# A feed-forward layer as five blocks of seven products, with the plain unit inside the first

## The chip, the cores and the metric
The kernel runs on one core of a Trainium2 chip. The metric is the device time of one execution in microseconds: the median of three runs before is 913.37 us (912.84 to 914.23). Time is also read from one execution recorded by the hardware profiler.

## What is computed
Two layers over 256 tokens of width 1024. Each layer has a SwiGLU feed-forward network (FFN), a mixer (an mLSTM in layer 0, windowed attention in layer 1) and a second FFN, each followed by a layer norm over the scaled residual. Everything is fp32. The part that matters here is the FFN, above all the last of the four:

```
def swiglu(x, w_in, w_out):          # x 256 x 1024, w_in 1024 x 5632, w_out 2816 x 1024
    gu = x @ w_in
    g, u = gu[..., :D_FF], gu[..., D_FF:]
    return (jax.nn.silu(g) * u) @ w_out
...
x = layer_norm(ALPHA * x + 0.5 * swiglu(x, ffn_w_in[l, 1], ffn_w_out[l, 1]), ln_g[l, 2], ln_b[l, 2])
```

## The kernel before
**Precision.** Every matmul operand is split into a high and a low part. ScalarE rounds a weight piece (128 x 1024 numbers) to the high part (`w_hi`), VectorE subtracts to get the low part (`w_lo`); both come from the raw piece in `w_raw` or `s_raw`. A product is then three matmuls: high by high, high by low, low by high (`mm3`, line 617). The tokens' side (x transposed, `xT_hi` and `xT_lo`) stands in the array, the weights stream through with 512 columns. The weights can be split at most `RING` = 10 pieces ahead.

**An FFN in 11 units.** The 2816 hidden columns are 11 units of 256. Before, each FFN does the first two units plainly (512 columns of g and 512 of u: 96 matmuls, eight pieces, each used for both token halves), then one unit plainly (`beside`: 256 columns of g next to 256 of u in one piece: 48 matmuls, four pieces), then four blocks of two units each by a scheme of seven products (Strassen's). `down` multiplies a finished 128-row chunk of the hidden layer by one piece of `w_out`: 12 matmuls per chunk, into four PSUM banks `py` that stay open to the end; six chunks are left for the `tail`, in which the layer norm starts as the halves finish.

**A block of seven products.** The weight block is cut in halves by rows of x (0 to 511, 512 to 1023) and by g and u columns: b11 and b21 for g, b12 and b22 for u, each as two pieces. x is cut by tokens and by columns; four sums of x (S1 to S4, `x_sum`, line 845) are made once per FFN. A block needs, in the order in which TensorE uses them: b11 (with x itself), b21 (with x), t1 (b11 after one sum, with S1), t2 (after a second sum, with S2), b12 after a sum (with S3), b22 (with S4), b11 after a third sum (with x). That is 14 split pieces and 84 matmuls. The sums of weights are made partly by VectorE (`sum`, line 348, which adds one raw piece to another) and partly by DMA (`add`, line 121: POOL issues a transfer from DRAM that is added to the piece in place). The raw pieces of b11, b12, b22 lie in rooms `s_raw0` to `s_raw3`, two pieces per room, with b11 in `s_raw0` and `s_raw3` by turns. PSUM bank qa collects the products with x (tokens half 0), S2, S3 and at last x (half 1); it is copied or read between them.

**What sets the order.** The code that plans the pieces (line 492 and after) writes down the order in which pieces are split and the due times. When the kernel is built, a planner (`Paced`, `Weights.fill`, lines 65 and 376) follows the engines with its own estimates of time and puts each split, sum and late eviction at a place between the other instructions. On the chip the engines' queues are then fixed: every engine takes its instructions in the order in which they were built and waits by semaphores. SP issues the loads of weights in order; POOL issues the DMA additions in order, between its small arithmetic.

**At the border to the last FFN.** During the attention (`attn`, line 1335) the rooms `s_raw1` and `s_raw2` hold the attention's probabilities and `s_raw3` its keys. The second token half of x is normalised late; `pending()` transposes it into xT once it is ready, so the FFN begins with token half 0 and calls `pending()` after 42 of its matmuls. S1 to S4 need both halves.

Of the kernel before, what the change touches and what calls it, by code (L numbers as in the profile page):

```python
# [21 lines left out]
F = 2816  # L22
UNITS = F // 256
SEVENS = 4
RAW_BUFS = 4
S_RAW = 2
# [162 lines left out]
class Weights:  # L189
# [5 lines left out]
    def __init__(self, nc, pool, rooms, words, plan, after):  # L195
        self.nc, self.pool, self.rooms, self.words, self.plan, self.after = nc, pool, rooms, words, plan, after
        self.raw, self.parts, self.half, self.sums = {}, {}, [], []
        self.made, self.used, self.gone, self.left = set(), 0, 0, 0
        self.todo = {tag: [i for i, w in enumerate(words) if w["tag"] == tag] for tag in TAGS}
        self.free = {"v_raw": 0, **{tag: S_RAW for tag in TAGS}, "w_raw": RAW_BUFS}  # L200
        self.spool, self.send, self.span = None, 0, FIRST
        self.later, self.fresh, self.owed, self.landed = [], None, 0, False
        self.uses = [0] * len(words)
# [19 lines left out]
    def load(self, most=None):  # L223
# [4 lines left out]
        while most is None or n < most:  # L228
            next_ = []
            for tag, todo in self.todo.items():  # L230
                if not todo:
                    continue
                first = self.first[todo[0]]
                if tag != "w_raw":
                    if self.free[tag] and not once and first < self.used + self.span:
# [209 lines left out]
def trunk_kernel(ctx: ExitStack, tc: tile.TileContext, x, ffn_w_in, ffn_w_out, ln_g, ln_b, ml_w_in, ml_gate_b,  # L445
# [45 lines left out]

    def seven(w, c0, c1, n, down):

# [5 lines left out]
        b21 = at(512, c0)  # L499
        full = n < SEVENS - 1  # L500
# [24 lines left out]

    ends = {}
    for j, (kind, l, i, _) in enumerate(stages):
        if kind == "ffn":
# [6 lines left out]

            for c0 in (0, F):
                for a in range(4):
                    wide(wi, a * 256, c0)
            for a in range(4):
                beside(wi, a * 256, 512, F + 512)  # L540
            down(2)
            for g in range(SEVENS):
                c0 = 768 + 512 * g
                seven(wi, c0, F + c0, g, down)
            down(6)
# [224 lines left out]
    def ffn(l, i, n, pending, last):  # L770
        with ExitStack() as ph:
# [96 lines left out]

            hB = h_room(4)
            chunks(hB, 4)  # L870
            hB0 = hB
            if start:
                sg = {}
# [71 lines left out]

            def seven(full, before):

# [36 lines left out]
                product(qa, of(0, 0), True, end1)  # L984
                before()
                if not full:
                    gb.extend(load_ln(lambda name: W.room(name, TAGS[1]), l, n))
# [5 lines left out]
                down(1)  # L993
                product(qa, sum_("S3"), False, end7)
                product(qb, sum_("S4"), False, end3)
                if full:
                    down(1)
                product(qa, of(4, 1), False, end4)
                if full:
                    down(1)  # L1000
# [6 lines left out]

            ps = [wbank(), wbank()]
            pieces = []
            for a in range(4):  # L1010
                pieces.extend(W.take(1))
                for t in range(2):
                    for k in (2 * a, 2 * a + 1):
                        mm3(ps[t], pair(xT, A, k, tok(t)), pair(pieces[a], A, k % 2), k == 0, k == 7)
                W.done()
                if not start:
                    for n_, f_ in zip(XP[1:], (x_three, x_two, x_four)):
                        if a == n_:
                            f_()
                if a == 1:  # L1020
                    for t in range(0 if start else 1, 2):
                        tr(hB0, t, hs[t])
            hh = []
            for t in range(2):
                sg = temp("sg")[:, 0:256]
                nc.scalar.activation(sg, ps[t][:, 0:256], AF.Silu)
                hh.append(temp("hh")[:, 0:256])
                nc.vector.tensor_mul(hh[t], sg, ps[t][:, 256:512])
            hp = h_room(2)
            chunks(hp, 2)  # L1030
            down(1)

            def turn():
                p = wbank((128, 2, S))
                for t in range(2):
                    for k in range(2):
                        nc.tensor.transpose(p[:, k, tok(t)], hh[t][:, k * 128:(k + 1) * 128], ident)
                split_evac(hp, p, wait=True)

            down(1)  # L1040
            for g in range(SEVENS):
                turn = seven(g < SEVENS - 1, turn)
            if start:
# [7 lines left out]
            return tail(y, lambda c, t: pair(hT[c], A, tok(t)), (todo, todo), False, norm,  # L1051
                        last, 4, turn, TAGS[1])

# [281 lines left out]
    def attn(l, n, pending, last):  # L1335
        with ExitStack() as ph:
# [215 lines left out]
            for st in range(11):  # L1552
# [83 lines left out]
```

## Time and profile before

| what | value |
|---|---|
| median of three runs | 913.37 us |
| the profiled execution's own time | 913.42 us |
| its span, first to last instruction | 911.7 us |
| TensorE busy, share of the span | 902.5 us, 99% |
| VectorE busy | 804.4 us, 88% |
| ScalarE busy | 573.1 us, 63% |
| POOL busy | 152.5 us, 17% |
| granted TensorE clock, mean | 0.999 |

In the rows, PE is TensorE's matmuls, PEld its weight loads, DVE is VectorE, ACT ScalarE, SP the engine that issues loads. A row of the timeline gives the start and the length in us, then engine, line, operation, output and inputs, shape, and how many instructions of that kind follow each other; in brackets the idle time before it and what ended it. A row of stretches gives, for a stretch of time, the busy time and the count of PE, PEld, DVE, ACT and POOL, then the granted clock, the DMA engines' busy share and the GB/s moved. Nearly all instructions are recorded in one helper (`call`, line 179), so they stand under L180 and are told apart by the names of their tiles. Busy times of pipelined instructions overlap a little; the spacing of starts is what one more of them costs.

### The profile page before, as it was taken

The page shows a single profiled execution, that of the slowest core. Times are in us where ns is not written, and L with a number is a line of the kernel's source. Part 1 is how long each engine was busy: PE and PEld are TensorE (multiplying, and loading weights), DVE is VectorE, ACT ScalarE, POOL GpSimd, SP SyncE. Part 2 cuts the span into 40 slices and gives each one's busy share as a digit, 9 for nine tenths or more (in the row PEclk, how much of TensorE's full clock was granted, in tenths as well). Part 3 has the DMA queues.
Part 4 walks back from the last instruction along what each step waited for, and adds up shares of the span by engine and source line. Part 5 has one row for each costly group of instructions (what it writes and reads, how often), then busy time and mean ns, then how long its engine had stood idle before and what let it go on. Part 6 is the DMA issues. An engine that isn't in the chain of part 4 may idle for free.

```text
span 911.7 us, 12563 instructions
## 1 busy us (share of the span) xinstructions
PE 902.5 (99%) x4459; PEld 757.4 (83%) x4459; DVE 804.4 (88%) x971; ACT 573.1 (63%) x793; POOL 152.5 (17%) x192
## 2 busy tenths in 40 slices
PE   9999999999999999999999999999999999999996
PEld 7888888889988888888888888888898888888885
DVE  5999999886799898999888899998869889899886
ACT  5776777356664656776646676764569566676660
POOL 0111123113211011212011111110425301111110
PEclk9999999999999999999999999999999999999999
DMA  8999998546637898997868989986534587899851
GB/s 281 367 328 259 288 274 215 162 137 186 208 111 246 296 234 244 290 285 234 241 193 269 259 257 283 272 223 197 159 119 140 163 293 221 204 298 278 252 138 47
DMA packets 100703, 208.53 MB, mean 229 GB/s; under 512 B 6904, under 2 KB 21264, under 8 KB 100640
## 3 DMA queue, kind: packets, MB, share of 16 engines
q1 hardware_dynamic: 82368, 173.04, 54.2%
q0 software_dynamic: 17696, 33.65, 22.3%
q10 hardware_dynamic: 576, 1.05, 0.3%
q8 instruction: 35, 0.57, 0.3%
q14 instruction: 28, 0.23, 0.1%
HBM read 206.65 MB, written 1.05 MB: 228 GB/s over the span
## 4 chain that ended last, share of the span: by engine, by line
PE 98%; DVE 1%; DMA 0%; issue 0%; DVEq 0%
PE pw L180 64%; PE py L180 35%; DMA x<-in_x_dram 0%; DVE x L180 0%; DVE stats L180 0%; DVEq L1632 0%; DVE mv L180 0%; DVE rs L180 0%
## 5 line engine op out<-in xcount | busy, mean ns | idle before, releaser
L180 DVE TENSOR_TENSOR w_lo<-w_raw,w_hi 128x1024 fp32r<-128x1024 f32 (+1 forms) x213 | 255.2, 1219 | 26.6 <-ACT w_hi L180 24.8
L180 ACT CAST w_hi<-w_raw 128x1024 fp32r<-128x1024 f32 (+1 forms) x213 | 218.9, 1049 | 80.3 <-PE py L180 21.7
L180 DVE TENSOR_TENSOR w_lo<-s_raw,w_hi 128x1024 fp32r<-128x1024 f32 x192 | 228.6, 1219 | 18.3 <-ACT w_hi L180 18.2
L180 ACT CAST w_hi<-s_raw 128x1024 fp32r<-128x1024 f32 x192 | 196.6, 1054 | 58.4 <-PE py L180 23.3
L180 PE MATMUL pw<-w_hi,xT_hi 128*128 128x512 f32 x480 | 189.5, 396 | 0.0
L180 PE MATMUL pw<-w_hi,xT_lo 128*128 128x512 f32 x480 | 187.0, 391 | 0.0
L180 PE MATMUL pw<-w_lo,xT_hi 128*128 128x512 f32 x480 | 186.7, 390 | 0.0
L122 POOL DMA_DIRECT2D s_raw<-in_ffn_w_in_dram x64 | 77.4, 1211 | 484.1 <-DVE s_raw L180 226.3
L180 PE MATMUL py<-w_hi,h_hi 128*128 128x512 f32 x349 | 138.2, 396 | 0.0
L180 PE MATMUL py<-w_hi,h_lo 128*128 128x512 f32 x349 | 136.2, 390 | 0.0
L180 PE MATMUL py<-w_lo,h_hi 128*128 128x512 f32 x349 | 136.0, 390 | 0.0
L180 PEld LDWEIGHTS pw<-w_hi,xT_lo 128*128 128x128 f32 x480 | 90.0, 188 | 19.1
L180 PEld LDWEIGHTS pw<-w_lo,xT_hi 128*128 128x128 f32 x480 | 90.3, 188 | 18.6 <-DVE w_lo L180 1.2
L180 PEld LDWEIGHTS pw<-w_hi,xT_hi 128*128 128x128 f32 x480 | 90.1, 188 | 17.4 <-ACT w_hi L180 0.2
L180 PE MATMUL pw<-w_hi,S_hi 128*128 128x512 f32 x256 | 99.7, 390 | 0.0
L180 PE MATMUL pw<-w_lo,S_hi 128*128 128x512 f32 x256 | 99.7, 389 | 0.0
L180 PE MATMUL pw<-w_hi,S_lo 128*128 128x512 f32 x256 | 99.7, 389 | 0.0
L180 PEld LDWEIGHTS py<-w_hi,h_lo 128*128 128x128 f32 x349 | 65.5, 188 | 14.1
L180 DVE TENSOR_TENSOR s_raw<-s_raw,s_raw 128x1024 f32<-128x1024 f32 x64 | 76.8, 1219 | 0.3
L180 PEld LDWEIGHTS py<-w_lo,h_hi 128*128 128x128 f32 x349 | 65.7, 188 | 13.0
L180 PEld LDWEIGHTS py<-w_hi,h_hi 128*128 128x128 f32 x349 | 65.6, 188 | 12.7
L180 PEld LDWEIGHTS pw<-w_hi,S_lo 128*128 128x128 f32 x256 | 48.1, 188 | 10.0
(205 smaller groups left out, 1122.7 us busy)
## 6 DMA issues: line engine op xcount, KB each, us to landing
s_raw<-in_ffn_w_in_dram SPq DMA_DIRECT2D x96, 512.0 KB, 8.0
w_raw<-in_ffn_w_out_dram SPq DMA_DIRECT2D x88, 512.0 KB, 6.1
w_raw<-in_ffn_w_in_dram SPq DMA_DIRECT2D x64, 512.0 KB, 5.7
s_raw<-in_ffn_w_in_dram POOLq DMA_DIRECT2D x64, 512.0 KB, 8.3
w_raw<-in_ml_w_in_dram SPq DMA_DIRECT2D x24, 512.0 KB, 4.6
w_raw<-in_ffn_w_in_dram SPq DMA_DIRECT2D x32, 256.0 KB, 6.0
w_raw<-in_at_w_in_dram SPq DMA_DIRECT2D x12, 512.0 KB, 4.8
w_raw<-in_ml_w_out_dram SPq DMA_DIRECT2D x8, 512.0 KB, 4.1
```

Of the source, the lines that this page charges most:

```text
L122: self.nc.gpsimd.dma_start(ap, source, accum_op=OP.add)
L180: r = f(out, *args, **kw)
```

## The change
Only the last FFN changes (stage 5, `FIVE`). Its hidden columns are taken as one plain 256-column unit and five blocks of seven products; the plain 512-column unit is gone. The plain unit no longer stands ahead of the blocks: it is `inner`, called within the first block between its second product (b21) and its third (S1), first for token half 0, with `pending()` in it, then for token half 1. The four sums of x are made in `inner` too, one after each quarter of token half 1 (`XF`). The transposes of the plain unit's result (`before()`), which in other blocks follow the first product, stand in this block after the product with S3, and right behind them the first `down`; the second follows the product with S4.

In the first block of the last FFN (`MOVED1`) the first sum of b11 is no longer made by VectorE from the b12 piece but by a DMA addition of the same columns from DRAM; b12's own addition then comes after t1's sum. The first block's b11 is loaded, split and added to during the attention. `W.lent` holds back loads into `s_raw1` and `s_raw2` while the attention uses these rooms. The result of the plain unit for both token halves lies in one 512-column temporary instead of two, and the last normalisation's g and b are loaded into the rooms `s_raw3` instead of `s_raw0`.

```diff
+FIVE = (5,)
+MOVED1 = ((5, 0),)
+XF = [0, 1, 2, 3]
...
         for j in range(2):
-            after[s1[j]] = [(b11[j], b12[j]), (b12[j], at(512, c1)[j])]
+            after[s1[j]] = [(b11[j], at(0, c1)[j] if (count, n) in MOVED1 else b12[j])]
+            if (count, n) not in MOVED1:
+                after[s1[j]].append((b12[j], at(512, c1)[j]))
...
-        down(1)
+        (inner or (lambda: down(1)))()
         t1 = [split_of(w_, None, p, half, BY_SUM) for w_, p in zip(b11, s1)]
         for j in range(2):
             after[t1[j]] = [(b11[j], b22[j])]
+            if (count, n) in MOVED1:
+                after[t1[j]].append((b12[j], at(512, c1)[j]))
...
+                for g in range(5):
+                    c0 = 256 + 512 * g
+                    seven(wi, c0, F + c0, g, down, 5, inner if g == 0 else None)
...
                 product(qa, of(0, 0), True, end1)
-                before()
+                if inner is None:
+                    before()
...
                 product(qc, of(4, 0), True, end2)
-                down(1)
+                if inner is None:
+                    down(1)
+                else:
+                    inner()
                 qb = wbank()
                 product(qb, sum_("S1"), True, end5)
                 product(qa, sum_("S2"), False, end6)
-                down(1)
+                if inner is None:
+                    down(1)
                 product(qa, sum_("S3"), False, end7)
+                if inner is not None:
+                    before()
+                    down(1)
                 product(qb, sum_("S4"), False, end3)
                 if full:
                     down(1)
                 product(qa, of(4, 1), False, end4)
-                if full:
+                if full and inner is None:
                     down(1)
...
+            def inner():
+                pieces = []
+                for t in range(2):
+                    ps = wbank()
+                    for a in range(4):
+                        if t == 0 and 2 * a == PEND[bound[0] - 1]:
+                            pending()
+                        if t == 0:
+                            pieces.extend(W.take(1))
+                        for k in (2 * a, 2 * a + 1):
+                            mm3(ps, pair(xT, A, k, tok(t)), pair(pieces[a], A, k % 2), k == 0, k == 7)
+                        if t == 1:
+                            W.done(W.used - 4 + a + 1)
+                            for n_, f_ in zip(XF, (x_one, x_three, x_two, x_four)):
+                                if a == n_:
+                                    f_()
+                    gated(t, ps)
...
+            W.lent = TAGS[2:4]
...
+            W.lent = ()
+            W.load()
```

More of the change, by code (lines that the diff above doesn't have):

```diff
@@ L234, in load @@
                 if tag != "w_raw":
-                    if self.free[tag] and not once and first < self.used + self.span:
+                    if self.free[tag] and tag not in self.lent and not once and first < self.used + self.span:
                         next_.append((first, tag, tag))
@@ L490, in rows, with seven @@
         piece(w[c * 128:(c + 1) * 128, :].rearrange("(k p) f -> p k f", p=128), 1, scale)
-    def seven(w, c0, c1, n, down):
+    def seven(w, c0, c1, n, down, count, inner=None):
         def at(r0, c):
@@ L499, in seven @@
         b21 = at(512, c0)
-        full = n < SEVENS - 1
+        full = n < count - 1
         half = 1360.0
@@ L944, in ffn, with seven @@
             gb = []
-            def seven(full, before):
+            def seven(full, before, inner=None):
                 of = lambda k0, t: (lambda k: pair(xT, A, k0 + k, tok(t)))
@@ L998, in seven @@
                 product(qa, of(4, 1), False, end4)
-                if full:
+                if full and inner is None:
                     down(1)
@@ L1006, in seven, with gated @@
                 return second
[L1008 to L1022, printed above, removed]
             hh = []
-            for t in range(2):
+            def gated(t, ps):
+                if t == 0:
+                    hh.append(temp("hh"))
                 sg = temp("sg")[:, 0:256]
[L1026 to L1031, printed above, removed]
+                nc.scalar.activation(sg, ps[:, 0:256], AF.Silu)
+                s_ = slice(256 * t, 256 * t + 256)
+                nc.vector.tensor_mul(hh[0][:, s_], sg, ps[:, 256:512])
             def turn():
@@ new lines, in ffn @@
+            if five:
+                hp = h_room(2)
+                chunks(hp, 2)
+            else:
+                ps = [wbank(), wbank()]
+                pieces = []
+                for a in range(4):
+                    pieces.extend(W.take(1))
+                    for t in range(2):
+                        for k in (2 * a, 2 * a + 1):
+                            mm3(ps[t], pair(xT, A, k, tok(t)), pair(pieces[a], A, k % 2), k == 0, k == 7)
+                    W.done()
+                    if not start:
+                        for n_, f_ in zip(XP[1:], (x_three, x_two, x_four)):
+                            if a == n_:
+                                f_()
+                    if a == 1:
+                        for t in range(0 if start else 1, 2):
+                            tr(hB0, t, hs[t])
+                for t in range(2):
+                    gated(t, ps[t])
+                hp = h_room(2)
+                chunks(hp, 2)
+                down(1)
+                down(1)
@@ L1043, in ffn @@
+            count = 5 if five else SEVENS
+            for g in range(count):
+                turn = seven(g < count - 1, turn, inner if five and g == 0 else None)
             if start:
```

49 lines of the change are left out of this document (30 added, 19 removed).

## The prediction
> **What bounds the kernel now.** I read the first part of the page (busy shares), then the chain of work that ended last, then the chain in order of time for the pace of one matmul, then the table of stretches and TensorE's waits over the last FFN, since only that FFN changes.
>
> ```profile
> span 911.7 us, 12563 instructions
> PE 902.5 (99%) x4459; PEld 757.4 (83%) x4459; DVE 804.4 (88%) x971; ACT 573.1 (63%) x793; POOL 152.5 (17%) x192
> PE 98%; DVE 1%; DMA 0%; issue 0%; DVEq 0%
> 56.70 5.44 PE pw L180 x24
> 729.50:887.00 157.50, 157.50 (x717) 130.46 (x717) 145.84 (x151) 103.97 (x124) 20.85 (x17) 1.00 0.85 244
> PEld pw L180 <- issue: 0.3, 2, 0.2
> ```
>
> TensorE is the chain: 98% of it, and from 729.5 to 887 us (the last FFN up to its tail) it is busy throughout; the only wait that TensorE's weight loads show from 700 us on is 0.3 us of issue. So a matmul taken away is a gain in full and a stall is a loss in full. One 512-column matmul costs 5.44 / 24 = 0.2267 us. The same row of the last FFN shows what is close behind: VectorE is busy 145.84 of 157.50 us, only 11.7 us idle. ScalarE (103.97) has room.
>
> **What goes: 12 matmuls.** A plain unit is 2 token halves x 2 column blocks x 8 rows of x x 3 = 96 matmuls, a block of seven products 7 x 4 x 3 = 84. Transposes are as many as before, and the built order of TensorE is 12 instructions shorter. Gain: 12 x 0.2267 = 2.72 us.
>
> **What comes on VectorE.** From the end of the attention's normalisation (the second `x<-x,rs,ln_b`) to the last `w_lo`, I count VectorE's built order by kind: 82 splits (`w_lo`) and 16 sums of 1024 columns before, 88 and 18 after (a block has 14 pieces where the unit had 8; of its four sums of weights two, those with b12, become DMA additions), and three 512-column steps more (five evictions for the two of the unit).
>
> ```profile
> 736.43 1.28 DVE L180 SCALAR_TENSOR_TENSOR x<-x,rs,ln_b 128x1024 f32<-128x1024 f32 x1
> 737.63 2.35 DVE L180 TENSOR_TENSOR w_lo<-w_raw,w_hi 128x1024 fp32r<-128x1024 f32 x2
> 808.31 4.62 DVE L180 TENSOR_TENSOR w_lo<-s_raw,w_hi 128x1024 fp32r<-128x1024 f32 x4
> 812.85 2.35 DVE L180 TENSOR_TENSOR w_lo<-w_raw,w_hi 128x1024 fp32r<-128x1024 f32 x2
> 762.07 0.69 DVE L180 TENSOR_TENSOR S_lo<-S,S_hi 128x512 fp32r<-128x512 f32 x1
> 762.67 0.68 DVE L180 TENSOR_TENSOR h_lo<-pw,h_hi 128x512 fp32r<-128x512 f32 x1
> 765.87 0.75 DVE L180 TENSOR_TENSOR hh<-sg,pw 128x256 f32<-128x256 f32 x2 [0.18 <-ACT sg L180]
> ```
>
> Back to back, one step of 1024 columns takes (812.85 - 808.31) / 4 = 1.135 us, one of 512 takes 0.60 (762.07 to 762.67), one of 256 about 0.35. Added: 8 x 1.135 + 3 x 0.60 = 10.9 us, against 11.7 us idle before. In total it fits, barely; so the question is where in time it falls. [...]
>
> **Where it falls: the first block.** Before, the plain 512-column unit gave VectorE and ScalarE 96 matmuls in which few pieces were due. Now the first block's sums, the four sums of x (S1 to S4) and the plain 256-column unit all stand in the first 20 us. The built order of VectorE is the same as before up to the row at 736.43, so the next step starts at 737.63 in both.
>
> ```profile
> 729.55 0.39 PE L180 MATMUL pw<-w_hi,xT_hi 128*128 128x512 f32 x1
> 739.07 1.04 PE L180 MATMUL py<-ident,x 128*128 128x128 f32 x8
> 746.79 0.60 PE L180 MATMUL pw<-ident,hh 128*128 128x128 f32 x4
> 747.14 0.48 PE L180 MATMUL pw<-w_hi,xT_hi 128*128 128x512 f32 x1
> ```
>
> TensorE: 42 matmuls from 729.55, eight transposes at 739.07, 30 matmuls, as before; the weights for them are as early as before. So at 746.79 the first block begins its product with S1 (12 matmuls, to 749.51), and at 749.51 the product with S2 is due, with the twice-summed b11 pieces (t2). With no stall S3 would be due at 752.23, the four transposes at 754.95, the first down product from 755.30 to 758.02.
>
> VectorE has ahead of the first t2 `w_lo`, by the built order: two `w_lo` (t1), the first eviction, two halves of xT, a sum, a 256 product, S1, a sum, S1_lo, S3, S2, the first down piece, S3_lo, S2_lo, S4, a 256 product, S4_lo, the first b22 piece, then t2 itself. That is 7 x 1.135 + 11 x 0.60 + 2 x 0.35 = 15.25 us: t2's first `w_lo` is ready at 752.9 at the earliest, and TensorE's second matmul of the product needs it at 749.74. **At least 3.2 us of stall**, whatever ScalarE does.
>
> ```profile
> 728.88 2.96 ACT L180 CAST w_hi<-w_raw 128x1024 fp32r<-128x1024 f32 x3
> 739.71 1.08 ACT L180 CAST xT_hi<-py 128x512 fp32r<-128x512 f32 x2 [0.78 <-PE py L180]
> 740.33 1.29 DVE L180 TENSOR_TENSOR xT_lo<-py,xT_hi 128x512 fp32r<-128x512 f32 x2 [0.35 <-ACT xT_hi L180]
> 750.52 0.69 DVE L180 TENSOR_TENSOR S<-x,py 128x512 f32<-128x512 f32 x1 [0.58 <-ACT x L180]
> 751.24 0.62 ACT L180 CAST S_hi<-S 128x512 fp32r<-128x512 f32 x1 [0.75 <-DVE S L180]
> ```
>
> ScalarE spaces splits by 0.955 us and 512-column steps by 0.49; a step that waits for another engine starts 0.03 to 0.05 us after that one's end (750.52 + 0.69 to 751.24). Its order after holds the four S_hi, a SiLU and the copy of S1's product ahead of t2's `w_hi`, and S4_hi waits for VectorE's S4. Laid out with these spacings: xT_hi ends at 740.7, S4 at 749.96, S4_hi at 750.5, the SiLU and the copy at 751.3, t2's first `w_hi` at 752.35, its `w_lo` at 754.2. The product with S2 runs from 752.4 with a gap to 754.3 and ends at 756.8. The second b12 piece is five splits behind t2 on VectorE (759.9), so the product with S3 ends at 761.1. The four transposes of the inner unit then stand right before the down product: h_hi is behind four more splits on ScalarE (762.5), h_lo behind three steps on VectorE (763.4). The down product ends at 765.7 where 758.02 was due: **7.7 us of stall**. If ScalarE never held anything up, VectorE's order alone gives t2 752.9, the second b12 piece 758.6, h_lo 762.2: 6.5 us. I take 7.7; the ends are 6.0 and, with the late transfers below, 10.
>
> **After the first block.** A full block gives VectorE 18 splits, 4 sums and 7 steps of 512: 22 x 1.135 + 7 x 0.60 = 29.2 us, and TensorE 132 matmuls and eight transposes: 29.9 + 0.8 = 30.7 us. VectorE gains 1.5 us a block on TensorE and doesn't lose more; I add 0, with 0 to 2 for a piece that is late in the second block, where I find it 1 to 2 us ahead.
>
> **The queues.** SP issues as many loads as before; two of them (`s_raw`) move ahead into the attention stage between loads of its output weights, where the DMA share is 0.55 and then 0.46, so the transfers hide. Two DMA additions move with them onto POOL.
>
> ```profile
> 700.00:715.00 15.00, 15.00 (x112) 13.03 (x112) 12.16 (x30) 11.64 (x36) 9.17 (x18) 1.00 0.55 168
> 715.00:729.50 14.50, 14.50 (x78) 12.39 (x76) 12.43 (x18) 7.27 (x10) 1.53 (x1) 1.00 0.46 157
> ...
> 709.62 1.22 DVE L180 TENSOR_TENSOR w_lo<-w_raw,w_hi 128x1024 fp32r<-128x1024 f32 x1
> 711.45 0.20 POOL L1485 TENSOR_TENSOR sm<-sm,es 128x4 f32<-128x4 f32 x1 [1.72 <-ACT es L180]
> 712.84 1.84 POOL L1489 TENSOR_SCALAR sc<-sc,sm 128x256 f32<-128x256 f32 x4
> 714.62 1.04 PE L180 MATMUL pw<-ident,sc 128*128 128x128 f32 x8
> 754.72 1.24 POOL L122 DMA_DIRECT2D s_raw<-in_ffn_w_in_dram  x1 [18.91 <-ACT w_hi L180]
> s_raw<-in_ffn_w_in_dram SPq DMA_DIRECT2D x96, 512.0 KB, 8.0
> s_raw<-in_ffn_w_in_dram POOLq DMA_DIRECT2D x64, 512.0 KB, 8.3
> ```
>
> The second addition waits for the split at 709.62 (ends 710.84), holds POOL 1.2 us, and behind it stands the scaling of the last pair of heads, which began at 711.45: 0.6 us later. The transposes at 714.62 follow the last scaling (to 714.68) with no room, so 0.4 to 0.6 of it reaches TensorE; I take 0.5 (0 to 1.2). The other four additions of the block (two for b12 from about 736, two for b11 from about 755) land some 8.3 us later, before their splits at 753 and 763 to 765. The second block's first b12 load can issue only at 756.5, when its room is given back, and with 8.0 us to land it comes at 764.5, 1.2 us behind VectorE's 763.3: 0 taken, 1.3 the bound. The gated product kept in one 512-column temporary and the normalisation's g and b in other rooms cost nothing: they are the same steps on the same engines, and g and b, issued in the last block, are read only in the tail.
>
> **Sum**, against the profiled execution's own 913.42 us (0.05 above the median of 913.37): -2.72 + 7.7 + 0.5 = +5.5, so **918.9 us**, 0.6% slower. Low end -2.72 + 6.0 + 0 = +3.3 (916.7); high end -2.72 + 7.7 + 1.2 + 1.3 + 2 = +9.5 (922.9).
>
> **Rivals.**
> - *The gain alone arrives* (other side): 913.42 - 2.72 = 910.7 us. It needs t2's first split 3.2 us sooner than VectorE's order allows, for instance work that I put behind 737.63 done before it. For it: before, ScalarE waits for TensorE to free rooms in the stretch (below), so the planner runs ahead where it can. Against: queues are in order and the 15.25 us are rows. It decides where the sum ahead of t2 is under 12.1 us. Chance 0.07.
> - *Only the S2 wait counts*: b12 and h_hi turn out on time, stall 3.2 to 4.7 us, sum -0.5 to +2: 912.9 to 915.4. Against it: both stand behind more splits. Chance 0.07.
> - *VectorE or the additions stay behind in later blocks*: each block then adds 1 to 2 us, +10 to +14: 923 to 927. For it: the last FFN now has 22 additions through POOL's queue where it had 16, and VectorE has hardly any idle left. Against: 1.5 us a block to spare. Chance 0.12.
> - *TensorE's clock falls in the gaps*.
>
> ```profile
> 742.90 1.05 ACT L180 CAST w_hi<-w_raw 128x1024 fp32r<-128x1024 f32 x1 [2.12 <-PE pw L180]
> 905.00:911.00 6.00, 0.00 (x0) 0.00 (x0) 3.59 (x8) 0.00 (x0) 0.92 (x1) 0.91 0.23 87
> ```
>
> After the last matmul (none from 905 on) the granted clock is 0.91 over six microseconds, so about 1 us of them at half: it takes some 5 us idle here. My longest gap is 2.9 us. If a gap did it, 3.4 us at half pace would lose 1.7 us: 920.6. Chance 0.04. [...]
>
> **Numbers.** My forecast (916.7 to 922.9) 0.70; the rest as above. Range 915.5 to 923.5. A measurement of this kernel tells about 0.2% (1.8 us) from no change: slower by more 0.88 (the forecast, the later blocks, the clock and a little of the second rival), within 0.05 (the rest of that rival), faster 0.07 (the gain alone).
>
> **What the changed profile would show.** TensorE's instructions 12 fewer; weight loads of the last FFN waiting for `w_hi` and `w_lo` some 6 us in all, and for h_hi and h_lo 1 to 2 us, between 749 and 764; VectorE without idle from 737 to 765; the sc transposes 0.5 us later; afterwards an unbroken chain. The prediction is wrong if the t2 split comes before 750, if the blocks after the first wait too, or if the stall lies in a DMA's landing.

## The result and the profile after

The changed kernel takes 924.3 us (median of three runs, 923.86 to 925.88) against 913.37 us: 1.0123 times as long, 95% interval 1.0100 to 1.0146. It is slower, as predicted, but by 10.9 us where 5.5 were forecast, and 924.3 lies above the range (915.5 to 923.5).

From the page of the changed kernel: the span, the busy times, the chain that ended last.

```profile
span 922.6 us, 12576 instructions
PE 905.4 (98%) x4447; PEld 757.3 (82%) x4447; DVE 815.4 (88%) x982; ACT 580.6 (63%) x802; POOL 160.9 (17%) x198
PE 89%; DVE 6%; issue 1%; DMA 1%; ACT 1%; POOL 1%; DVEq 0%; ACTq 0%; POOLq 0%
```

TensorE has the 12 instructions fewer (4459 to 4447), VectorE is 11.0 us busier (10.9 were worked out). But TensorE is no longer the whole chain: 98% became 89%, and VectorE has 6%. TensorE's timeline of the changed kernel at the places that matter:

```profile
740.71 1.04 PE L183 MATMUL py<-ident,x 128*128 128x128 f32 x8
754.09 0.49 PE L183 MATMUL pw<-w_hi,S_hi 128*128 128x512 f32 x1 [2.78 <-ACT w_hi L183]
755.99 0.79 PE L183 MATMUL pw<-w_lo,S_hi 128*128 128x512 f32 x1 [1.41 <-DVE w_lo L183]
...
761.78 0.50 PE L183 MATMUL pw<-w_hi,S_hi 128*128 128x512 f32 x1 [0.73 <-ACT e L183]
...
766.57 0.50 PE L183 MATMUL py<-w_hi,h_hi 128*128 128x512 f32 x1 [1.33 <-ACT h_hi L183]
...
769.72 0.39 PE L183 MATMUL pw<-w_hi,S_hi 128*128 128x512 f32 x1
...
806.86 0.50 PE L183 MATMUL pw<-w_lo,xT_hi 128*128 128x512 f32 x1 [1.65 <-DVE w_lo L183]
...
915.31 0.28 PE L183 MATMUL pw<-w_hi,h_lo 128*128 128x256 f32 x1
```

The transposes of x are 1.64 us later than before (739.07 to 740.71 for the second half of the tokens). The product with S2 waits for its t2 piece twice, with one matmul between. The row at 755.99 is new in kind: 0.79 us for a matmul that otherwise shows 0.39. A stretch tells why (columns: time, then busy time and count of PE, PEld, DVE, ACT, POOL, then the granted clock, the DMA share, GB/s):

```profile
754.70:761.40 6.70, 5.06 (x11) 3.47 (x11) 6.70 (x7) 4.32 (x6) 2.42 (x2) 0.50 0.75 162
```

For 6.7 us TensorE's granted clock is one half; the eleven matmuls left of the product with S2 take 5.06 us instead of 11 x 0.2267 = 2.49. VectorE ahead of that stretch, in it, and at the second block's late piece:

```profile
752.64 0.42 DVE L183 TENSOR_TENSOR hh<-sg,pw 128x256 f32<-128x256 f32 x1 [0.97 <-ACT sg L183]
...
753.59 5.76 DVE L183 TENSOR_TENSOR w_lo<-s_raw,w_hi 128x1024 fp32r<-128x1024 f32 x5
...
760.40 1.22 DVE L183 TENSOR_TENSOR w_lo<-s_raw,w_hi 128x1024 fp32r<-128x1024 f32 x1
763.23 2.36 DVE L183 TENSOR_TENSOR w_lo<-s_raw,w_hi 128x1024 fp32r<-128x1024 f32 x2 [1.62 <-ACT w_hi L183]
...
799.72 1.23 DVE L183 TENSOR_TENSOR s_raw<-s_raw,s_raw 128x1024 f32<-128x1024 f32 x1 [0.79 <-DMA s_raw<-in_ffn_w_in_dram]
```

The second of the five splits from 753.59 on is t2's first `w_lo`. Ahead of it VectorE waited 0.97 us for ScalarE at 752.64, so the stall is not VectorE's steps alone. The second b12 piece is ready at 761.62, just ahead of where the slowed product lets S3 begin; then VectorE itself is idle for 1.62 us, since ScalarE's queue stood behind that product's copy. And POOL in the attention, where the two additions stand (four scalings of sc took 1.84 us before, a single one 0.48):

```profile
706.43 1.24 POOL L125 DMA_DIRECT2D s_raw<-in_ffn_w_in_dram  x1 [1.95 <-ACT es L183]
707.25 0.67 POOL L1548 TENSOR_TENSOR sm<-sm,es 128x4 f32<-128x4 f32 x1
...
709.12 2.90 POOL L1552 TENSOR_SCALAR sc<-sc,sm 128x256 f32<-128x256 f32 x4
709.58 1.53 POOL L1552 TENSOR_SCALAR sc<-sc,sm 128x256 f32<-128x256 f32 x1
709.63 1.21 DVE L183 TENSOR_TENSOR w_lo<-s_raw,w_hi 128x1024 fp32r<-128x1024 f32 x1
711.97 1.20 POOL L125 DMA_DIRECT2D s_raw<-in_ffn_w_in_dram  x1
712.77 0.64 POOL L1548 TENSOR_TENSOR sm<-sm,es 128x4 f32<-128x4 f32 x1
```

The row at 709.58 is the second of the four scalings in the row above it, by itself. Both additions delay the scalings behind them, not only the second: an addition takes 1.24 or 1.20 us, and the small step behind it 0.67 or 0.64 instead of 0.20. Pushed back by the first addition, one scaling now stands beside VectorE's split at 709.63 and takes 1.53 us instead of 0.48; that makes the 2.90. Behind the second addition the four scalings took 1.84 us again. TensorE's transposes of sc show what reaches it, first in the kernel before, then in the changed one:

```profile
710.80 1.03 PE L180 MATMUL pw<-ident,sc 128*128 128x128 f32 x8
```

```profile
710.80 2.04 PE L183 MATMUL pw<-ident,sc 128*128 128x128 f32 x8
...
715.62 1.67 PE L183 MATMUL pw<-ident,sc 128*128 128x128 f32 x8
```

Of the 1.64 us, 1.01 come behind the first addition (2.04 instead of 1.03) and 0.63 behind the second (1.67 instead of 1.04).

### The profile page after: what moved, and what is told of

It is laid out like the page before. It is cut to its first block, busy times and chain, and to the rows that moved or that the text cites. A ratio compares the mean times of both kernels' runs of the same rounds, so it can differ in the third digit from the quotient of the medians.

```text
span 922.6 us, 12576 instructions
## 1 busy us (share of the span) xinstructions
PE 905.4 (98%) x4447; PEld 757.3 (82%) x4447; DVE 815.4 (88%) x982; ACT 580.6 (63%) x802; POOL 160.9 (17%) x198
## 3 DMA queue, kind: packets, MB, share of 16 engines
q10 hardware_dynamic: 576, 1.05, 0.3%
HBM read 209.79 MB, written 1.05 MB: 229 GB/s over the span
## 4 chain that ended last, share of the span: by engine, by line
PE 89%; DVE 6%; issue 1%; DMA 1%; ACT 1%; POOL 1%; DVEq 0%; ACTq 0%; POOLq 0%
PE pw L183 57%; PE py L183 31%; DVE w_lo L183 3%; DMA w_raw<-in_ffn_w_out_dram 1%; DVE x L183 1%; ACT w_hi L183 1%; DVE s_raw L183 1%; DVE stats L183 0%; POOL sc L1552 0%; DVE S_lo L183 0%; DVE S L183 0%; DVE xT_lo L183 0%; DVE e L183 0%; POOL rs L721 0%; DVE h_lo L183 0%
## 5 line engine op out<-in xcount | busy, mean ns | idle before, releaser
L183 DVE TENSOR_TENSOR w_lo<-w_raw,w_hi 128x1024 fp32r<-128x1024 f32 (+1 forms) x207 | 247.8, 1218 | 24.6 <-ACT w_hi L183 22.9
L183 DVE TENSOR_TENSOR w_lo<-s_raw,w_hi 128x1024 fp32r<-128x1024 f32 x204 | 242.3, 1217 | 15.0 <-ACT w_hi L183 15.0
L183 ACT CAST w_hi<-s_raw 128x1024 fp32r<-128x1024 f32 x204 | 208.8, 1054 | 58.3 <-DVE s_raw L183 22.2
L183 PE MATMUL pw<-w_hi,xT_hi 128*128 128x512 f32 x460 | 181.4, 396 | 0.0
L183 PE MATMUL pw<-w_lo,xT_hi 128*128 128x512 f32 x460 | 178.6, 390 | 1.7 <-DVE w_lo L183 1.7
L183 PE MATMUL pw<-w_hi,xT_lo 128*128 128x512 f32 x460 | 179.0, 390 | 0.0
L125 POOL DMA_DIRECT2D s_raw<-in_ffn_w_in_dram x70 | 84.7, 1212 | 489.1 <-DVE s_raw L183 221.6
L183 PE MATMUL pw<-w_hi,S_hi 128*128 128x512 f32 x272 | 106.8, 392 | 3.5 <-ACT w_hi L183 2.8
L183 PE MATMUL pw<-w_lo,S_hi 128*128 128x512 f32 x272 | 106.9, 393 | 1.4 <-DVE w_lo L183 1.4
L183 PEld LDWEIGHTS pw<-w_hi,S_hi 128*128 128x128 f32 x272 | 51.5, 189 | 15.4 <-ACT w_hi L183 3.2
```

What stands on the lines that cost most here:

```text
L125: self.nc.gpsimd.dma_start(ap, source, accum_op=OP.add)
L183: r = f(out, *args, **kw)
```

## The experiments

Three causes were to be told apart: VectorE's queue ahead of t2, the fall of the clock, POOL's queue in the attention; later a fourth, the second block's late piece. Each run stood beside runs of the kernel before on the same chip (medians 913.37 to 913.81); "over before" is the difference to those, 10.9 us for the changed kernel. Its 95% interval is about 1.4 us to either side (2.1 for the changed kernel itself), so differences of 1 to 2 us between two versions are read from their traces and not from the medians alone. The profiled executions begin the last FFN up to 1.9 us apart, in code that most of the edits don't touch, so places in them are counted from the transposes of x's second half (740.71 in the changed kernel; 174.60 us from there to the last matmul at 915.31, and 165.32 in the kernel before).

### The gaps at S2 filled with idle transposes

```diff
+            def keep(n):
+                p = wbank((128, 4, 128))
+                for j in range(n):
+                    nc.nc.tensor.transpose(p[:, j % 4], ident, ident)
...
                     w, = W.take(1)
+                    if j == 0 and busy and busy[0]:
+                        keep(busy[0])
...
+                            nc.tensor.matmul(bank, x_of(0)[0], w[0][:, 0], start=False, stop=False, skip_group_check=True)
+                            keep(busy[1])
...
-                product(qa, sum_("S2"), False, end6)
+                product(qa, sum_("S2"), False, end6, (20, 10) if inner else None)
```

The second run has (20, 0).

> The changed kernel with 20 idle transposes of the identity on TensorE ahead of the first matmul with S2 and 10 ahead of its second; the order of every other engine is unchanged. Theory (the clock is a loss of its own, set off by the two gaps): the granted clock stays at 1.00 from 754 to 762 us, the last 11 matmuls with S2 take 2.5 us instead of 5.07, the second b12 piece (its w_lo at 761.6) becomes the next wait, and the time falls by 1.8 to 2.6 us, to about 922.1. Rival (the half pace only fills time in which the pieces for S3 and h_hi were late anyway): 923.6 or more.

> As the run before, with the 20 transposes alone: the gap of 2.78 us is filled, the one of 1.41 us after the first matmul with S2 stays. If the gap of 1.41 us alone pulls the clock down, the time is that of the changed kernel, 924.3. If it takes both gaps or the longer one, the clock stays at 1.00 and the time is that with both gaps filled, about 922.1.

Both gaps filled: 922.57 us, 8.8 over before (ratio 1.0096, 1.0081 to 1.0111), so 2.2 us gained by the medians. In the trace, from the transposes at 741.32 to the last matmul at 913.65 it takes 172.33 us, 2.27 less. TensorE's rows and its clock:

```profile
754.71 0.50 PE L183 MATMUL pw<-w_hi,S_hi 128*128 128x512 f32 x1 [0.61 <-ACT w_hi L183]
756.62 0.50 PE L183 MATMUL pw<-w_lo,S_hi 128*128 128x512 f32 x1 [0.32 <-DVE w_lo L183]
760.14 0.50 PE L183 MATMUL pw<-w_hi,S_hi 128*128 128x512 f32 x1 [0.73 <-ACT e L183]
762.30 0.50 PE L183 MATMUL pw<-w_lo,S_hi 128*128 128x512 f32 x1 [0.26 <-DVE w_lo L183]
...
768.16 0.39 PE L183 MATMUL pw<-w_hi,S_hi 128*128 128x512 f32 x1
```

```profile
751.00:764.00 13.00, 11.09 (x63) 8.52 (x61) 12.03 (x14) 11.56 (x15) 2.42 (x2) 1.00 0.75 198
```

The pieces come when they came (756.62 - 741.32 = 15.30, against 755.99 - 740.71 = 15.28), the clock stays at 1.00, and the first down product ends at 768.16, 26.84 us after the transposes instead of 29.01. So the fall of the clock cost 2.2 us, and the wait that takes its place is the second b12 piece, small (0.26). With the first gap alone filled it is 922.61 us, 8.8 over before: the median of both gaps filled, which by the expectation would be a clock at 1.00. But its trace has the clock fall all the same, in a shorter stretch:

```profile
755.60:758.90 3.30, 3.30 (x9) 2.60 (x8) 3.30 (x4) 2.42 (x3) 2.32 (x2) 0.50 0.80 191
```

From the transposes to the last matmul that execution gains 1.2 us, not 2.3; the two medians, with their intervals, can't tell these apart. Ahead of this fall stood the gap of 1.41 us, with 0.61 us before it.

### POOL's additions after the attention

```diff
-            self.transfer(*sums.pop(0)[1:])
+            if self.lent:
+                self.held.append(sums.pop(0)[1:])
+            else:
+                self.transfer(*sums.pop(0)[1:])
...
             W.lent = ()
+            for a in W.held:
+                W.transfer(*a)
```

> The two DMA additions of the first block that stand on POOL among the attention's scalings are issued after the last scaling instead; the loads stay where they are. Theory (POOL's queue costs 1.64 us): the transposes of sc are back at 714.6, those of the first x at 727.3 instead of 728.9, and the time falls by 1.6 us to 922.7. Rival (the two loads moved into the attention, or their traffic, cost it): the transposes stay at 728.9 and the time at 924.3.

924.24 us, 10.4 over before (1.0114, 1.0099 to 1.0129): next to nothing gained. Yet the saving is there at its place. TensorE's rows, POOL's row and two stretches of this kernel (the clock is the third number from the end):

```profile
739.26 1.04 PE L183 MATMUL py<-ident,x 128*128 128x128 f32 x8
...
805.16 0.50 PE L183 MATMUL pw<-w_lo,xT_hi 128*128 128x512 f32 x1 [2.09 <-DVE w_lo L183]
```

```profile
714.83 2.43 POOL L125 DMA_DIRECT2D s_raw<-in_ffn_w_in_dram  x2
```

```profile
754.60:757.90 3.30, 3.30 (x8) 2.62 (x9) 3.30 (x4) 2.74 (x3) 2.42 (x2) 0.50 0.70 173
805.80:809.10 3.30, 3.30 (x11) 2.69 (x10) 1.95 (x3) 1.58 (x3) 0.00 (x0) 0.50 1.07 356
```

From the attention's transposes before the additions (706.59 in the changed kernel, 706.78 here) those of x come 1.64 us sooner, and the first down product, at 764.44, is 2.3 us sooner (the clock is low for one stretch, not two). Then the second block's piece waits 2.09 instead of 1.65 us, and this time the clock falls there too: half pace for 3.4 us, 1.7 us lost. In this execution the gain was real and was spent on a second fall.

### The down product ahead of S2

```diff
+        if inner is not None:
+            down(1)
         t2 = [split_of(w_, None, p, half, BY_SUM) for w_, p in zip(b11, t1)]
...
                 product(qb, sum_("S1"), True, end5)
+                if inner is not None:
+                    before()
+                    down(1)
                 product(qa, sum_("S2"), False, end6)
                 product(qa, sum_("S3"), False, end7)
-                if inner is not None:
-                    before()
-                    down(1)
```

> The four transposes of the gated product and the first down product stand between the products with S1 and S2 instead of after S3; its w_out piece is split one place earlier. Theory (VectorE's queue ahead of t2 makes the gap, so other work of TensorE fits into it): the wait for t2 vanishes, replaced by about 1.8 us for hh and 1 to 2 us for h_hi and h_lo, the clock stays near 1.00, and the copy of S2's product is the only wait after it: 3 to 5 us faster, about 920.3. Rival (VectorE is full over the whole block, so what is gained at S2 is lost at S4 or at the last product): 923 or more.

923.79 us, 10.0 over before (1.0113, 1.0096 to 1.0130). In its trace the clock stays up (0.998 in the mean) and t2's wait is gone, but the rival's number came: VectorE is behind for the whole block, and the loss moves to the waits for `hh` and h_hi and to the last product of that block (a wait of 1.78 us stays in the second block).

```profile
752.77 0.44 PE L183 MATMUL pw<-ident,hh 128*128 128x128 f32 x2 [1.61 <-DVE hh L183]
754.22 0.50 PE L183 MATMUL py<-w_hi,h_hi 128*128 128x512 f32 x1 [1.01 <-ACT h_hi L183]
...
771.63 0.50 PE L183 MATMUL pw<-w_lo,xT_hi 128*128 128x512 f32 x1 [1.82 <-DVE w_lo L183]
775.04 0.50 PE L183 MATMUL pw<-w_lo,xT_hi 128*128 128x512 f32 x1 [1.75 <-DVE w_lo L183]
```

> The down product between S1 and S2 together with the additions after the attention's last scaling. If the parts add, 923.79 - 1.64 = 922.1 us, unless one of the four waits of 1.6 to 1.8 us, which now fall otherwise on the clock's steps, takes the clock down: each fall would cost up to 1.7 us. If VectorE's queue and the transfers set the pace of both blocks from the attention's end on, the saving of 1.64 us stays, since both start 1.64 us earlier.

Both edits together: 921.85 us, 8.4 over before (1.0093, 1.0077 to 1.0109); 922.1 was expected. Here the 1.64 us stay, though the clock fell once, at 752.5 us (0.996 in the mean).

### VectorE's queue shortened

```diff
-                split_evac(xs[name], f, wait=True)
+                if five:
+                    hi = xs[name][0]
+                    nc.scalar.copy(hi, f)
+                    xs[name] = (hi, hi)
...
+                else:
+                    split_evac(xs[name], f, wait=True)
```

> The changed kernel without the four steps S_lo of the last FFN: the products with S1 to S4 take the high half in place of the low one, so that part of the computation is left out; all else stands in the same order on every engine. Theory (the sum of VectorE's steps ahead of t2 sets the stall): t2's first w_lo comes 4 x 0.60 = 2.4 us earlier, so the second matmul with S2 starts 2.4 us earlier than 755.99, at 753.6 by the time base of the changed kernel; its w_hi at 752.3; the clock stays at 1.00, and the first down product starts 3.5 to 4.5 us earlier. The time falls by as much less what the second block takes back: if that block's late piece is set by transfers that don't move, its wait of 1.65 us grows by 1 to 3 us. Rival (ScalarE or a DMA holds t2): the second matmul stays within 0.7 us of 755.99.

922.91 us, 9.4 over before (1.0108, 1.0093 to 1.0124). The rows are from the slowest of its four executions, which took 925.39 us:

```profile
741.90 1.04 PE L183 MATMUL py<-ident,x 128*128 128x128 f32 x8
...
755.37 0.79 PE L183 MATMUL pw<-w_lo,S_hi 128*128 128x512 f32 x1 [0.77 <-DVE w_lo L183]
...
765.26 0.50 PE L183 MATMUL py<-w_hi,h_hi 128*128 128x512 f32 x1 [1.30 <-ACT h_hi L183]
...
806.34 0.62 PE L183 MATMUL pw<-w_lo,xT_hi 128*128 128x512 f32 x1 [2.46 <-DVE w_lo L183]
```

```profile
754.09 4.63 DVE L183 TENSOR_TENSOR w_lo<-s_raw,w_hi 128x1024 fp32r<-128x1024 f32 x4 [0.51 <-ACT w_hi L183]
```

Taking 2.4 us of VectorE away brings t2's second matmul to 13.47 us after the transposes instead of 15.28: 1.8 us earlier, where the rival allowed 0.7. VectorE's queue sets most of the stall. Of the 2.4 us, 0.6 don't arrive, because VectorE now waits 0.51 us for ScalarE's `w_hi` of that piece: ScalarE's queue stands close behind. The clock fell here too (1.62 and 0.77 us of waiting), so the first down product gains 2.5 us, not the 3.5 to 4.5 expected. And in this execution the second block takes it back: 2.46 us of wait and another fall; it ends as late after the transposes as the changed kernel's (174.50 us).

Done by GpSimd instead of being left out (`nc.gpsimd.tensor_sub` for the four steps):

> The four steps S_lo of the last FFN done by GpSimd instead of VectorE; nothing left out. The planner then lays the pieces out a little differently (t2's first piece is three places earlier on ScalarE, the second b12 piece as far behind as before). By the theory of VectorE's queue t2's first w_lo comes about 2.4 us earlier and the second b12 piece at best 1 us earlier: S2 starts near 752, S3 waits for b12, and the time falls by 1 to 2.5 us (921.8 to 923.3). If GpSimd's steps take over 1.5 us each or slow VectorE, nothing is gained.

929.0 us, 15.5 over before (1.0170, 1.0155 to 1.0185): far worse. The rows of POOL and VectorE, from the fastest of its four executions (927.95 us):

```profile
749.32 4.19 POOL L873 TENSOR_TENSOR S_lo<-S,S_hi 128x512 fp32r<-128x512 f32 x3
```

```profile
747.93 1.73 DVE L183 TENSOR_TENSOR w_lo<-w_raw,w_hi 128x1024 fp32r<-128x1024 f32 x1
...
752.28 2.33 DVE L183 TENSOR_TENSOR w_lo<-s_raw,w_hi 128x1024 fp32r<-128x1024 f32 x1
```

GpSimd takes 1.4 us a step, and two of VectorE's splits beside these steps grow (1.73 and 2.33 for 1.22). So 1.6 of the 2.4 us that VectorE gave away are lost on VectorE again, and the clock fell twice in the first block, at 755.5 and 765.7 us. The order of the pieces differs here too, so the 4.6 us more than in the changed kernel are not taken apart further.

### The second block's late piece

The four DMA additions of the second block left out, then VectorE's four sums of weights (the planner is told their time as before, so that it lays out the rest alike):

```diff
+        if (count, n) == (5, 1):
+            SKIP.update(b11 + b12)
...
+        if w in SKIP:
+            nc.moving(1, t, ARRIVING, ADDING, SENDING)
+            return
```

```diff
-        nc.vector.tensor_add(t, t, self.raw[v])
+        if w in SKIP:
+            nc.on_vector("tensor_add", 1024, [t], [t, self.raw[v]])
+        else:
+            nc.vector.tensor_add(t, t, self.raw[v])
```

> The changed kernel without the four DMA additions of the second block (POOL's queue moves 2 MB less; the sums they would make are left out); the order of all other instructions is unchanged. If the late piece of the second block (the wait of 1.65 us at 806.86) is a matter of transfers under contention or of an addition landing late, the wait goes and the time falls by 1.5 to 1.8 us to about 922.6. If it is a matter of VectorE's full queue, the wait stays within 0.4 us of 1.65.

> The changed kernel without VectorE's four sums of weights in the second block (4.5 us of VectorE; the sums are left out); the order of all other instructions is unchanged. If VectorE's full queue makes the second block's wait, it goes and the time falls by 1.5 to 1.8 us to about 922.6. If transfers make it, a load whose room comes free only after such a step is issued somewhat earlier and the wait shrinks by less than 1 us.

923.75 us without the additions (10.3 over before), 924.57 without the sums (11.1). The waits were 0.78 and 1.77 us, but the clock fell in both first blocks and in the second run also at 806.9 us (mean clocks 0.996 and 0.994), which hides what was asked. So the same with the gaps at S2 filled:

> The kernel with both gaps at S2 filled, and without the four DMA additions of the second block (their sums left out). There the late piece of the second block waited 1.22 us with the clock at 1.00. If transfers make it late, the wait falls to 0.3 us or less and the time by 0.9 to 1.2 us from 922.57 to about 921.5. If VectorE does, it stays above 0.9.

> The kernel with both gaps at S2 filled, and without VectorE's four sums of weights in the second block (4.5 us of VectorE, left out). If VectorE's full queue makes the second block's late piece, the wait of 1.22 us goes and the time falls to about 921.4. If transfers do, it stays above 0.8 us and the time within 0.5 us of 922.57.

921.01 and 920.77 us, 7.6 and 7.4 over before, against 8.8 with both in place. The wait fell from 1.22 to 0.76 and 0.82 us (0.75 and 0.86 us less from the transposes to the last matmul). The first is neither of its two expectations; in the second the wait is that of the transfers and the time that of VectorE's queue. Then neither additions nor sums:

> The kernel with both gaps at S2 filled, and without both the four DMA additions and VectorE's four sums of the second block (both left out). Without the additions alone the late piece waited 0.76 us, without the sums alone 0.82, with both in place 1.22. If VectorE's load and the transfers share the wait, it is gone without either (under 0.2 us). If ScalarE or the first block's late start alone makes the piece late, 0.5 us or more remain.

921.34 us, 7.7 over before (1.0087, 1.0070 to 1.0104). No less than with one left out: the wait is still 0.76 us. VectorE's rows there (no DMA wait left), and TensorE's:

```profile
798.31 0.68 DVE L184 TENSOR_TENSOR e<-pw,e 128x512 f32<-128x512 f32 x1
799.02 0.69 DVE L184 TENSOR_TENSOR e<-e,e 128x512 f32<-128x512 f32 x1
799.63 2.35 DVE L184 TENSOR_TENSOR w_lo<-w_raw,w_hi 128x1024 fp32r<-128x1024 f32 x2
801.91 3.49 DVE L184 TENSOR_TENSOR w_lo<-s_raw,w_hi 128x1024 fp32r<-128x1024 f32 x3
```

```profile
797.95 0.39 PE L184 MATMUL py<-w_hi,h_hi 128*128 128x512 f32 x1
...
803.18 0.50 PE L184 MATMUL pw<-w_lo,xT_hi 128*128 128x512 f32 x1 [0.76 <-DVE w_lo L184]
```

This floor is the built order, as far as the rows show; no run moved the piece. The late piece's `w_lo` stands behind the eviction of the product with S4: from that product's end (about 798.2) VectorE does two steps of 512 and three of 1024, to 803.13. TensorE has one down product and seven matmuls in that time, 19 x 0.2267 = 4.3 us from 797.95, and is done at 802.4. VectorE isn't late there: the eviction begins as the product ends. The rest of the wait is VectorE's own wait for a transfer ahead of that same eviction: 0.79 us in the changed kernel (the row at 799.72 above), and in the kernels with both gaps filled and with the additions late:

```profile
798.06 1.23 DVE L183 TENSOR_TENSOR s_raw<-s_raw,s_raw 128x1024 f32<-128x1024 f32 x1 [0.34 <-DMA s_raw<-in_ffn_w_in_dram]
```

```profile
798.01 1.23 DVE L183 TENSOR_TENSOR s_raw<-s_raw,s_raw 128x1024 f32<-128x1024 f32 x1 [1.21 <-DMA s_raw<-in_ffn_w_in_dram]
```

To VectorE's 0.34, 0.79 and 1.21 us belong waits of the late piece of 1.22, 1.65 and 2.09. In the 11 traces of changed kernels with this order of pieces and no idle transposes there, the late piece waits 0.76 to 0.88 us longer than VectorE does for that transfer. Without the additions VectorE's wait is gone in every trace, so the additions make this part. Without the sums alone it is gone with the gaps filled, but 0.92 us where the clock fell (there the late piece waited 1.77); why the sums bear on it at times stays open.

### The clock held and the additions late

The first two edits together, and 14 idle transposes ahead of the second block's late piece:

> The changed kernel with three edits together: the first block's two additions after the attention's last scaling, the 20 and 10 idle transposes ahead of the first and second matmul with S2, and 14 idle transposes ahead of the late piece of the second block. Theory (the parts add: POOL's queue 1.64 us, the half pace 1.7 us for each step of 3.41 us, and late additions alone only moved the loss into a second fall of the clock at 805 us): no fall of the clock anywhere, the late piece of the second block stays a wait of 1.5 to 2.5 us partly filled, and the time is 921.0 (920.3 to 921.8). Rival (the second block gives back whatever the first gains, clock or not): 922.3 or more.

920.18 us, 6.8 over before (1.0073, 1.0057 to 1.0089), 0.1 below the expected range. The clock is 1.00 throughout (one row over both blocks):

```profile
745.00:815.00 70.00, 67.24 (x322) 54.58 (x321) 68.19 (x72) 49.18 (x59) 12.07 (x10) 1.00 0.93 267
```

It gains 4.2 us on the changed kernel: the parts do add once the clock can't take them back. No version beats the kernel before; what is left is the stall of the first block, 7.9 us and so larger than the 2.72 us gained, and some 1.5 us in the second.

## Why the prediction was right or wrong

Against 10.9 us (the spans, 911.7 to 922.6), by the prediction's own terms:

| term | predicted | measured |
|---|---|---|
| 12 matmuls fewer | -2.72 | -2.72 |
| POOL's delay of the scaling | +0.5 (0 to 1.2) | +1.64 |
| stall of the first block, clock held | +7.7 (6.0 to 10) | +7.9 |
| the clock in the gaps | rival, +1.7, chance 0.04 | +2.2 |
| after the first block, transfers | 0 (to 2, and to 1.3) | +1.9 |

- **The first block: right.** The orders of VectorE and ScalarE together gave the second matmul with S2 at 754.3 (VectorE's alone 752.9); with the 1.64 us of the later start that is 755.9, and it came at 755.99. The second b12 piece was put at 759.9, so 761.5, and came at 761.62. With the clock held, the first down product ends 26.84 us after the transposes of x, where the working has 765.7 - 739.07 = 26.63; that is the 7.9. The run without S_lo shows that VectorE's queue sets most of it, and ScalarE's the 0.6 us that didn't arrive.
- **The clock: the step that failed most.** The rival was named and priced, and given 0.04, because "it takes some 5 us idle here. My longest gap is 2.9 us." That 5 us was read from the end of the kernel, after the last matmul, and was not the same in both kernels: in the changed one the same idle end brought the clock down after 2.9 us (last section). The longest gap was 2.8 us and the clock fell. The gap of 1.41 us with one matmul between was also in the forecast's own working; the two were never added up. Single waits of 1.77 us (the second block without the sums) and 2.09 us (the additions late) came before a fall too. The 3.4 us of half pace in the rival's price stood in no row of the kernel before; the runs showed them, 754.52 to 757.94 with the additions late, and in the changed kernel twice as much, 754.67 to 761.49.
- **POOL: one half left out.** 1.64 for 0.5, and above its bound of 1.2. The second addition cost 0.63, close to the 0.5. The first was put at nothing without a reason, and cost 1.01: in the kernel before, the scalings ran from 707.88 to 709.72 and TensorE came to them at 710.80, so 1.1 us to spare, but the addition pushed their start back by 1.24 and set one of them beside a split of VectorE, where it took 1.05 us longer.
- **After the first block: mis-sized.** 1.9 where 0 was taken and 2 was the bound; 1.65 of it is one wait in the second block. The rival "VectorE or the additions stay behind in later blocks" (0.12) was true for one block of four. The piece "that is late in the second block, where I find it 1 to 2 us ahead" was worked out as sums over a block; it is late because a transfer came late ahead of the eviction of S4 (shown by the runs above) and, as its rows say, because of its place behind that eviction.
- **The signs and the range.** Waits of some 6 us for `w_hi` and `w_lo` and of 1 to 2 us for h_hi and h_lo were named; they were 4.2 us (2.78 and 1.41) and 1.3 us for h_hi, the third piece's wait being hidden by the half pace. VectorE without idle to 765 us was wrong: 0.97 us at 752.64, waiting for ScalarE, and, for the half pace, 1.62 us at 763.23. The signs named for error were the later blocks waiting and a stall in a DMA's landing, and both showed in the second block. The range took the terms to their bounds (+9.5), but the clock was a rival that stood alone and was never put on top of them.

The direction held because the stall alone is larger than the gain in matmuls.

## What to carry to other kernels

Add up the idle time that a change leaves on TensorE within a few us, waits on both sides of a lone matmul included, and price a fall of the clock with it: here 2.2 us for the 6.8 us at half pace after waits of 2.78 and 1.41 us, and an estimate of 1.7 us, half of it, for a low stretch of 3.4 us. A small gain may buy only another fall, as the 1.64 us of the late additions did, so fill such gaps with idle work when comparing versions, or the clock decides the comparison. And a work sum that fits over a block doesn't say that a piece is on time: look at what stands ahead of it in its engine's queue, and at what that waits for.

## What the runs showed of the hardware

The half pace came in stretches of 3.4 us or twice that. From the shares of the clock in stretches of 0.1 us, they ran from 754.67 to 761.49 in the changed kernel, and from 754.52 to 757.94 with the additions late. Where one execution had falls in both blocks they began 51.2 us apart (754.52 and 805.72), as did those of the run without S_lo (755.37 and 806.57); the two falls with GpSimd, 755.45 and 765.69, are 10.24 us apart, and in the changed kernel the fall after the last matmul, at 918.51, began 163.84 us after the first. That is 15, 3 and 48 times 3.41 us; what sets these places was not shown.

The length of one wait didn't tell whether the clock fell. Half pace followed waits of 2.78 and 1.41 us with one matmul between (the changed kernel), 1.62 and 0.77 in the same way (without S_lo), and single waits of 2.09 us (805.16, the additions late) and 2.46 us (806.34, without S_lo). But after 1.65 us in the changed kernel (806.86), after 1.82, 1.75 and 1.78 us with the down product ahead of S2, and after 2.25 us with GpSimd (810.51) the 512-column matmuls behind the waiting one took 0.39 or 0.40 us each, where those at half pace took 0.63. Nor did the idle end of the kernel. In the kernel before, the last matmul ends at 904.67 and the clock falls at 909.86, 5.2 us later; that is the forecast's 5 us. In the changed kernel it ends at 915.59 and the clock falls at 918.51, 2.9 us later. The clock was not back after a fixed stretch of work either: in the changed kernel the clock was low until 761.49, though eleven matmuls had followed one another from 755.99 on; with the additions late they began at 754.57, and the clock was back at 757.94. What exactly is counted stays open; no run varied a gap by itself.

Idle transposes kept the clock up here: with both gaps filled, 0.61 and 0.32 us of waiting are left beside them, and the clock stays at 1.00 from 751 to 764 us.

Executions of the same kernel differed in the clock. The four executions without S_lo had mean clocks of 0.997, 0.996, 0.994 and 0.994 and took 922.27, 922.37, 923.44 and 925.39 us. The three runs of the changed kernel all have 0.994, so their spread of 2.0 us (923.86 to 925.88) is not explained by this.

In two places a step of GpSimd and one of VectorE ran side by side and one of them took longer. A scaling on POOL took 1.53 us instead of 0.48 beside a split of VectorE (709.58), and a split of VectorE 2.33 us instead of 1.22 beside a step of GpSimd (752.28, the run with S_lo on GpSimd).
